# 1280 NO_OPs in the program of TensorE, one behind each group of three large matmuls

## Chip, core and metric

The kernel runs on one core of one Trainium2 chip. The metric is the device time of one execution in microseconds (us). TensorE is called PE below, its weight loads PEld, VectorE DVE, ScalarE ACT, GpSimd POOL and SyncE SP, as the profile does.

## What is computed

One step of a hybrid decoder layer, for 1024 new tokens of one prompt and 8 single new tokens of running sequences. All is float32, with D = 2048 features:

```python
mod = silu(c) @ w_ada + b_ada
shift, scale, gate = split(mod, 3)
h = rmsnorm(x, norm_g) * (1 + scale) + shift
z = h @ w_in                                    # 2048 x 8208
b_a, c_a, h_a, g_a, qkv, g_b, beta_logit, alpha_logit = split(z)
y_a = b_a * causal_conv3(c_a * h_a) * silu(g_a)
q, k, v = split(silu(causal_conv4(qkv)))        # 8 heads of 128, q and k of unit length
o, s = gated_delta_rule(q, k, v, g, beta, s0)   # g, beta from the logits
y = concat(y_a, rmsnorm(o, o_norm_g) * silu(g_b)) @ w_out
x = x + gate * y
```

The outputs are the final RMSNorm of x and the new states of the two convolutions and of the delta rule. Most of the arithmetic is in the two products with w_in and w_out.

## The kernel before

The features lie on the 128 partitions, the tokens on the free axis. The tokens are done in two halves: half 0 is 512 tokens of the prompt, half 1 the other 512 and the 8 single ones. In each half a loop first goes over the 64 column tiles (128 columns each) of w_in, in an order written out by hand (`order`), and then over the 16 column tiles of w_out. In half 1 the tokens are split into two blocks of 264 and 256.

A float32 product is made of three matmuls of a narrower kind (`float32r`). Each operand is split in two, a rounded part (hi) and what is left (lo); `passes` adds hi x hi, lo x hi and hi x lo into one accumulator tile in PSUM. Such a group of three matmuls, for one 128-row piece of the contraction and one block of tokens, is what the change speaks of. In the profile the activations of the products with w_in are called `hh` and `hl`, those with w_out `yhi` and `ylo`, and the weights `whi` and `wlo`. Each matmul has its own weight load in the chip's program, even where two in a row use the same weights.

`product` computes one column tile: 16 pieces of contraction, so 16 groups (48 matmuls) in half 0, and 32 groups in half 1 where there are two blocks. It takes the split weights from a stream (`ws.next`): SP loads 128x512 pieces (`raw`), ACT rounds them (`whi`), and POOL or DVE computes the rest (`wlo`). The first seven column tiles are computed elsewhere, in the phase that computes `mod`, and don't go through `product`.

Between the matmuls of a group `passes` calls `pump`, where small work of other generators is slipped in: transposes, the steps of the delta rule, the gate vectors. A planner (`_Order`) decides this while the kernel is built, from its own account of when each engine is free. That account is told of a matmul by the helper at line 369, `_Tensor.mm`; all matmuls carry line 370 in the profile, all other recorded operations line 321.

What is computed from a column tile leaves PSUM by ACT or DVE; an output tile of w_out in half 0 is read by DVE (`res<-mm,ga,xr`). There are three accumulator tiles (`ps_mm`), so the first matmul of a tile waits for an earlier reader of its place, and for the weights.

Of the kernel before, what the change touches and what calls it, by code (L numbers as in the profile page):

```python
# [77 lines left out]
def trunk_kernel(tc, xT, w_in, w_ada, w_out, pack, consts, vecs, csq, ssm,  # L78
                 yT, cap, cqp, ssp, cas, cqs, sss):
    nc = tc.nc  # L80
    ctx = ExitStack()
    with ctx:
        _trunk(ctx, tc, nc, xT, w_in, w_ada, w_out, pack, consts, vecs, csq, ssm, yT, cap, cqp, ssp, cas, cqs, sss)
# [6 lines left out]
class _Order:  # L90
# [156 lines left out]
    def pump(self):  # L247
        for s in list(self.side):
            if s[0] <= self.now:
                self._step(s)  # L250
# [112 lines left out]
class _Tensor:  # L363
# [5 lines left out]
    def mm(self, out, lhsT, rhs, cost=None, **kw):  # L369
        r = self.pe.matmul(out, lhsT, rhs, **kw)  # L370
        if cost is None:
            n = _size(rhs)
            if rhs.dtype == F32R:
                cost = max(n / 2250.0, 0.05) + 0.004
            elif kw.get("is_transpose"):
                cost = 0.109
            else:
                cost = max(4 * n / 2400.0, 0.21) + 0.006
        self.od.put("P", [lhsT, rhs], [out], cost)
        return r  # L380


def _trunk(ctx, tc, nc, xT, w_in, w_ada, w_out, pack, consts, vecs, csq, ssm, yT, cap, cqp, ssp, cas, cqs, sss):
# [18 lines left out]
    def mm_tile():  # L402
        return ps_mm.tile([P, 512], F32, tag="mm", name="mm")
# [231 lines left out]
    def passes(ps, whi, wlo, hh, hl, a, b, first, last, fill=False):  # L635
        mm(ps[:, :b - a], whi, hh[:, a:b], start=first, stop=False)
        if fill:
            pump()
        mm(ps[:, :b - a], whi, hl[:, a:b], start=False, stop=False)
        if fill:  # L640
            pump()
        mm(ps[:, :b - a], wlo, hh[:, a:b], start=False, stop=last)
        if fill:
            pump()

    def product(w, col, rows, ops, blocks, before=None):


        pss = [mm_tile() for _ in blocks]
        for qi, kq in enumerate(rows):  # L650
            if before:
                before(qi)
            whi, wlo = ws.next((col, kq), ws.used)
            for ps, (a, b) in zip(pss, blocks):
                for j in range(4):
                    hh, hl = ops[kq * 4 + j]
                    passes(ps, whi[:, j, :], wlo[:, j, :], hh, hl, a, b, qi == 0 and j == 0, qi == 3 and j == 3, True)
        return pss


# [599 lines left out]
    def group_a(half, g, blocks, y, pch=None):  # L1260
        n = WH if half else HT
        pc = pch[0] if pch else product(w_in, 1024 + g * P, range(4), hs, blocks)
        hold("ca", 1)
        c_ = tp.tile([P, WH], F32, tag="ca", name="c_", bufs=1)
        for ps, (a, b) in zip(pc, blocks):
            S.activation(c_[:, a:b], ps[:, :b - a], AF.Copy)
        phh = pch[1] if pch else product(w_in, 2048 + g * P, range(4), hs, blocks)
        hold("zr", 2)
        u = tp.tile([P, WH + 3], F32, tag="zr", name="ua")
# [24 lines left out]
        od.spawn(conv())  # L1294
        yield
        pg = pch[2] if pch else product(w_in, 3072 + g * P, range(4), hs, blocks)
        hold("ca", 1)
        gc = tp.tile([P, WH], F32, tag="ca", name="gc", bufs=1)
# [631 lines left out]
```

## Time and profile before

| | |
|---|---|
| time, median of 3 runs | 2162.79 us (2159.91 to 2165.25) |
| the profiled execution | 2164.96 us, span 2163.2 us |
| granted clock of PE, mean | 0.993 |
| PE busy | 2116.0 us, 15045 matmuls |
| PEld busy | 1853.8 us, 15045 weight loads |
| DVE, ACT, POOL busy | 1262.9, 826.3, 835.9 us |

The span goes from the first to the last instruction. The time of a matmul in a row is that of one matmul from its start to its modelled end; matmuls overlap, so how fast they follow each other is read from their starts. Behind a row of the timeline stands, in brackets, for how long the engine was idle and who ended that. PEldq is the sequencer of PE, which hands weight loads and matmuls to the array and carries out what needs no array.

### The profile page before, as it was taken

Reading aid. Unit: us, or ns where it says so; the run is one execution under the profiler, and the core shown is the slowest. Engines: PE = TensorE matmul, PEld = TensorE weight load, DVE = VectorE, ACT = ScalarE, POOL = GpSimd, SP = SyncE. Lnnn points to the kernel's source line nnn. Section 1 sums busy time; section 2 is a strip of 40 time slices with the busy share of each in tenths; the row PEclk is TensorE's granted clock in tenths of the full one; section 3 lists DMA queues with packets and bytes.
Section 4 is the critical chain, followed back from the end, with each engine's and each line's share of the span. In section 5 each row is a group of like instructions: output and inputs, shape, how many; then the busy total and the mean of one; then the engine's idle time right before and its main releaser. Section 6 shows DMA issues by size and latency. Waiting matters only on the chain. (4 is left out here: it accounts for less than half of the span.)

```text
span 2163.2 us, 40436 instructions
## 1 busy us (share of the span) xinstructions
PE 2116.0 (98%) x15045; PEld 1853.8 (86%) x15045; DVE 1262.9 (58%) x3646; ACT 826.3 (38%) x1885; POOL 835.9 (39%) x808
## 2 busy tenths in 40 slices
PE   9899999999999999999999999999999999999996
PEld 6478777777788887778899999999999999999996
DVE  3347776666768645287134865666576487245454
ACT  3234343334444332343233334342443433344553
POOL 0133433333343434323444334344443433444444
PEclk9999999999999999999999999999999999999998
DMA  9974765997445357855445565467574445868776
GB/s 313 340 220 83 161 149 147 134 165 134 115 99 98 89 104 83 82 182 179 142 102 120 107 120 119 113 100 104 107 93 90 89 103 95 92 92 241 228 208 197
DMA packets 466599, 299.66 MB, mean 139 GB/s; under 512 B 37601, under 2 KB 429537, under 8 KB 466401
## 3 DMA queue, kind: packets, MB, share of 16 engines
q1 hardware_dynamic: 442608, 284.26, 61.4%
q10 hardware_dynamic: 23792, 12.81, 2.4%
q8 instruction: 118, 1.93, 0.4%
q14 instruction: 81, 0.66, 0.1%
HBM read 277.06 MB, written 19.94 MB: 137 GB/s over the span
## 5 line engine op out<-in xcount | busy, mean ns | idle before, releaser
L321 POOL TENSOR_TENSOR wlo<-raw,whi 128x512 fp32r<-128x512 f32 x536 | 718.6, 1342 | 1222.7 <-ACT whi L321 1067.6
L370 PE MATMUL mm<-hh,whi 128*128 128x264 f32 (+1 forms) x3008 | 971.6, 323 | 10.9 <-DVE y L321 5.6
L370 PE MATMUL mm<-hl,whi 128*128 128x264 f32 (+1 forms) x3008 | 969.2, 322 | 3.7 <-DVE hl L321 3.7
L370 PE MATMUL mm<-hh,wlo 128*128 128x264 f32 (+1 forms) x3008 | 968.2, 322 | 0.7 <-POOL wlo L321 0.7
L321 ACT ACTIVATE whi<-raw 128x512 fp32r<-128x512 f32 x672 | 418.4, 628 | 617.7 <-PE mm L370 323.8
L370 PEld LDWEIGHTS mm<-hh,whi 128*128 128x128 f32 x3008 | 567.7, 189 | 61.6 <-issue 9.8
L370 PEld LDWEIGHTS mm<-hl,whi 128*128 128x128 f32 x3008 | 568.0, 189 | 47.7 <-DVE hl L321 5.9
L370 PEld LDWEIGHTS mm<-hh,wlo 128*128 128x128 f32 x3008 | 567.8, 189 | 43.6 <-issue 2.5
L370 PE MATMUL mm<-yhi,wlo 128*128 128x512 f32 (+2 forms) x768 | 247.7, 323 | 5.4 <-DVE wlo L321 3.2
L370 PE MATMUL mm<-yhi,whi 128*128 128x512 f32 (+2 forms) x768 | 246.6, 321 | 1.2 <-ACT whi L321 1.2
L370 PE MATMUL mm<-ylo,whi 128*128 128x512 f32 (+2 forms) x768 | 247.1, 322 | 0.0
L321 DVE TENSOR_TENSOR ob<-tb,xb 128x62 f32<-128x62 f32 (+30 forms) x992 | 191.5, 233 | 7.0 <-DMA tb<-ub 7.0
L321 DVE TENSOR_TENSOR xb<-xb,ob 128x62 f32<-128x62 f32 (+30 forms) x992 | 195.5, 237 | 0.0
L321 DVE TENSOR_TENSOR wlo<-raw,whi 128x512 fp32r<-128x512 f32 x136 | 108.2, 802 | 110.4 <-ACT whi L321 106.3
L370 PEld LDWEIGHTS mm<-yhi,wlo 128*128 128x128 f32 x768 | 145.3, 189 | 19.9 <-DVE wlo L321 4.8
L370 PEld LDWEIGHTS mm<-yhi,whi 128*128 128x128 f32 x768 | 145.3, 189 | 12.9 <-ACT whi L321 1.7
L370 PEld LDWEIGHTS mm<-ylo,whi 128*128 128x128 f32 x768 | 145.2, 189 | 12.5 <-issue 1.0
L321 DVE SCALAR_TENSOR_TENSOR kq<-zr,pk,kq 128x512 f32<-128x512 f32 x96 | 105.0, 1094 | 3.4
L321 DVE SCALAR_TENSOR_TENSOR res<-mm,ga,xr 128x512 f32<-128x512 f32 (+2 forms) x48 | 27.3, 568 | 106.1 <-PE mm L370 92.9
L321 DVE TENSOR_TENSOR acc<-acc,sqt 128x512 f32<-128x512 f32 (+3 forms) x70 | 51.3, 736 | 38.2 <-ACT sqt L321 37.3
L321 DVE SCALAR_TENSOR_TENSOR rt<-cht,gt_neg,v 128x128 f32<-128x128 f32 x56 | 19.5, 349 | 78.9 <-PE cht L370 78.8
L321 ACT ACTIVATE u<-cht,sm 128x128 f32<-128x128 f32 x64 | 23.5, 367 | 99.6 <-DVE u L321 95.7
(410 smaller groups left out, 1996.3 us busy)
## 6 DMA issues: line engine op xcount, KB each, us to landing
raw<-in_w_in SPq DMA_DIRECT2D x488, 256.0 KB, 5.1
raw<-in_w_out SPq DMA_DIRECT2D x160, 256.0 KB, 3.3
wat<-in_w_ada SPq DMA_DIRECT2D x64, 512.0 KB, 8.7
gw<-in_w_ada SPq DMA_DIRECT2D x64, 256.0 KB, 6.5
tb<-ub ACTq DMA_DIRECT2D x16, 512.0 KB, 6.1
raw<-in_w_in SPq DMA_DIRECT2D x48, 128.0 KB, 6.7
sl<-in_ssm SPq DMA_DIRECT2D x12, 512.0 KB, 6.1
x1s<-in_xT SPq DMA_DIRECT2D x16, 260.0 KB, 4.8
```

The costliest lines, as they stand in the source:

```text
L321: r = f(*args, **kw)
L370: r = self.pe.matmul(out, lhsT, rhs, **kw)
```

## The change

A list of 1280 entries is made once. In `product`, behind each group of three matmuls, one entry is taken and one instruction that does nothing is put into PE's program, until the list is empty.

```diff
+    spaces = [0] * 1280
+
     def product(w, col, rows, ops, blocks, before=None):
...
                 for j in range(4):
                     hh, hl = ops[kq * 4 + j]
                     passes(ps, whi[:, j, :], wlo[:, j, :], hh, hl, a, b, qi == 0 and j == 0, qi == 3 and j == 3, True)
+                    if spaces:
+                        spaces.pop()
+                        nc.tensor.nop("space", nofuse=True)
         return pss
```

The instruction goes to PE directly, past `_Tensor.mm`, so the planner doesn't know of it. Apart from these 1280 rows every engine has the same instructions in the same order with the same waits as before. Product groups of half 0 take 57 x 16 + 16 x 16 = 1168 of them, the first three and a half tiles of half 1 the other 112.

PE in half 0, in the first tile that goes through `product` (`mm`; the number tells one tile of a name from another, and `tpt` is a small transpose of the logits `zl`), before:

```order
L370 MATMUL mm_1633<-hl_879,whi_1506 128x512
L370 MATMUL tpt_1674<-cs_82,zl_1631 128x16 [waits Activation_49]
L370 MATMUL tpt_1674<-cs_82,zl_1631 128x16 x3
L370 MATMUL mm_1633<-hh_878,wlo_1507 128x512
L370 MATMUL mm_1633<-hh_1096,whi_1524 128x512
L370 MATMUL mm_1633<-hl_1097,whi_1524 128x512
L370 MATMUL mm_1633<-hh_1096,wlo_1525 128x512 [waits Pool_49]
```

The same place in the changed kernel:

```order
L370 MATMUL mm_1633<-hl_879,whi_1506 128x512
L370 MATMUL tpt_1681<-cs_82,zl_1631 128x16 [waits Activation_49]
L370 MATMUL tpt_1681<-cs_82,zl_1631 128x16 x3
L370 MATMUL mm_1633<-hh_878,wlo_1507 128x512
L662 NO_OP
L370 MATMUL mm_1633<-hh_1096,whi_1524 128x512
L370 MATMUL mm_1633<-hl_1097,whi_1524 128x512
L370 MATMUL mm_1633<-hh_1096,wlo_1525 128x512 [waits Pool_49]
L662 NO_OP
```

A NO_OP stands behind each matmul with `wlo` and in front of the next with `whi`; what `pump` slips in stays where it was.

PE in half 0 at the border between two output tiles of w_out, before:

```order
L370 MATMUL mm_10293<-ylo_9357,whi_10294 128x512
L370 MATMUL mm_10293<-yhi_9184,wlo_10295 128x512
L370 MATMUL mm_10374<-yhi_9183,whi_10316 128x512 [waits DVE_49,Activation_49]
L370 MATMUL mm_10374<-ylo_9196,whi_10316 128x512
L370 MATMUL mm_10374<-yhi_9183,wlo_10317 128x512 [waits Pool_49]
```

The same border in the changed kernel:

```order
L370 MATMUL mm_11365<-ylo_10277,whi_11366 128x512
L370 MATMUL mm_11365<-yhi_10080,wlo_11367 128x512
L662 NO_OP
L370 MATMUL mm_11462<-yhi_10079,whi_11392 128x512 [waits DVE_49,Activation_49]
L370 MATMUL mm_11462<-ylo_10092,whi_11392 128x512
L370 MATMUL mm_11462<-yhi_10079,wlo_11393 128x512 [waits Pool_49]
L662 NO_OP
```

The first matmul of a tile waits for two engines, DVE and ACT, as before; the NO_OP stands in front of it and waits for nothing.

PE in half 1, where the list runs out, in the changed kernel (before, the same rows without the NO_OP):

```order
L370 MATMUL mm_12606<-hh_10471,whi_12509 128x256
L370 MATMUL mm_12606<-hl_10472,whi_12509 128x256
L370 MATMUL mm_12606<-hh_10471,wlo_12510 128x256
L662 NO_OP
L370 MATMUL mm_12605<-hh_10707,whi_12548 128x264
L370 MATMUL mm_12605<-hl_10708,whi_12548 128x264
L370 MATMUL mm_12605<-hh_10707,wlo_12549 128x264 [waits Pool_49]
```

From the last row on the program of PE is that of before.

## Prediction

> **What bounds the kernel now.** I read the page first, then the busy time by stage, then the groups and the waits inside the stretch that gets the new instructions, then single instructions there. The page:
>
> ```profile
> span 2163.2 us, 40436 instructions
> PE 2116.0 (98%) x15045; PEld 1853.8 (86%) x15045; DVE 1262.9 (58%) x3646; ACT 826.3 (38%) x1885; POOL 835.9 (39%) x808
> PE   9899999999999999999999999999999999999996
> PEclk9999999999999999999999999999999999999998
> ```
>
> PE is busy in every slice, at its full granted clock; no other engine passes 58%. So anything that lengthens PE's stream reaches the end of the kernel nearly one for one, and anything that doesn't touch it costs nothing. The profiled execution took 2164.96 us, its span 2163.2 us and 1.8 us around it; that is 0.1% above the median of the three runs, 2162.79 us (2159.91 to 2165.25).
>
> The groups of matmuls in the stretch from 160 to 1108 us tell how many groups of three the change follows there:
>
> ```profile
> L370 PE MATMUL mm<-hh,wlo 128*128 128x512 f32 x912 | 365.6, 401 | 0.7 <-POOL wlo L321 0.7
> L370 PE MATMUL mm<-yhi,wlo 128*128 128x512 f32 x256 | 101.0, 395 | 1.9 <-DVE wlo L321 1.9
> ```
>
> Each group of three ends in one matmul with wlo, so 912 + 256 = 1168 of the 1280 instructions stand in the first half of the sequence, and 112 remain for the second: three and a half tiles of 32 groups. By stage (columns: length, then busy time of PE, of its weight loads, DVE, ACT, POOL, the clock, DMA), and the waits of PE from 164 to 1163 us, the first and the last of nine rows, 14 waits together:
>
> ```profile
> 164.20:1107.90 943.70, 934.06 (x4845) 741.68 (x4843) 581.70 (x1680) 356.77 (x802) 353.75 (x330) 1.00 0.62 127
> 1107.90:1163.00 55.10, 55.10 (x463) 54.91 (x463) 26.81 (x52) 27.68 (x65) 25.50 (x28) 1.00 0.38 91
> ...
> PE mm L370 <- DVE wlo L321: 1.9, 2, 1.7
> ...
> PE tpt L370 <- DVE os__8082 L321: 0.3, 1, 0.3
> ```
>
> In 998.8 us PE stands still for 9.6 us. The array is the limit here, not what feeds it.
>
> **The change part by part.** It removes and moves nothing: the order of every engine is as before, no matmul gets another wait, and the new instructions carry none. It adds 1280 instructions to the sequencer of PE, which hands weight loads and matmuls to the array. What counts is whether the sequencer has that time to spare, and whether such an instruction stops it from working ahead.
>
> First the array's pace. These are the last matmuls of one output tile and the first of the next, with the weight load of that first one and the eviction by DVE, which marks where the tile ends:
>
> ```profile
> 1031.44 0.40 PE L370 MATMUL mm<-yhi,whi 128*128 128x512 f32 x1
> 1031.67 0.40 PE L370 MATMUL mm<-ylo,whi 128*128 128x512 f32 x1
> ...
> 1035.38 0.39 PE L370 MATMUL mm<-yhi,wlo 128*128 128x512 f32 x1
> 1035.38 0.19 PEld L370 LDWEIGHTS mm<-yhi,whi 128*128 128x128 f32 x1
> 1035.61 0.40 PE L370 MATMUL mm<-yhi,whi 128*128 128x512 f32 x1
> 1035.81 0.75 DVE L321 SCALAR_TENSOR_TENSOR res<-mm,ga,xr 128x512 f32<-128x512 f32 x1 [8.29 <-PE mm L370]
> ```
>
> From 1031.44 to 1035.61 are 18 steps, 0.232 us each (the 0.40 us of a record overlaps with the next). The load at 1035.38 starts together with the matmul in front of it, so it is hidden. In the second half the products are split:
>
> ```profile
> 1203.02 0.28 PE L370 MATMUL mm<-hh,whi 128*128 128x264 f32 x1
> 1204.47 0.28 PE L370 MATMUL mm<-hh,whi 128*128 128x256 f32 x1
> 1205.90 0.28 PE L370 MATMUL mm<-hh,whi 128*128 128x264 f32 x1
> ```
>
> Twelve steps take 1.45 and 1.43 us, so 0.119 us for the narrower ones. A group of three lasts 0.696 us in the first half and at least 0.357 us in the second.
>
> Then the sequencer's pace. The fastest stream in the trace is the row of tiny warm-up matmuls, each with its weight load:
>
> ```profile
> 0.99 17.27 PE L370 MATMUL cht<-ones 32*32 32x32 f32 x320 [0.99 <-POOL nhalf L321]
> ```
>
> 17.27 / 320 = 0.054 us for a pair at most (the array may be what limits even this). Three pairs cost the sequencer up to 0.162 us. The trace has no NO_OP on PE. The nearest rows are another kind that the sequencer handles alone: the EVENT_SEMAPHOREs that stand in front of a matmul that waits for more than one semaphore (all of them, one at 1031.5, and four in a row just before the first output product):
>
> ```profile
> L370 PEldq EVENT_SEMAPHORE  x133: 51/51/399, 17.1 to 2092.0; - x133
> ...
> L370 PEldq EVENT_SEMAPHORE  x1: 51/51/51, 1031.5 to 1031.5; - x1
> ...
> L370 PEldq EVENT_SEMAPHORE  x4: 51/51/51, 919.3 to 919.7; - x4
> ```
>
> One lasts 0.051 us, and four stand within 0.4 us, so start to start is about 0.13 us. I take 0.051 us for a NO_OP, since it does less, and 0.13 us as the upper end. A group then costs the sequencer 0.213 us, at most 0.292, against 0.696 us of the array (0.357 in the second half). It stays faster than the array everywhere.
>
> The middle row says more. Of the output tiles here, only the first matmul waits for two things, for DVE and for ACT; its EVENT_SEMAPHORE ran at 1031.5 and the matmul itself at 1035.61. The sequencer was 17 matmuls, about 4 us, ahead, with 17 pairs queued behind it. So a sequencer's instruction runs while earlier matmuls are still waiting for the array, and a delay of 0.05 or 0.13 us is paid out of 4 us. **Cover:** those queued pairs hide the cost; where they are gone, right after PE had to wait at an EVENT_SEMAPHORE, a NO_OP could show. PE waits 14 times in the stretch: 14 x 0.13 = 1.8 us as the upper end. But behind such a wait the array first works through the pairs it was just given, so I take 0.1 us. The lower end is 0: no wait, load or matmul is dropped.
>
> Last, the program gets longer, and is fetched by DMA (packets, MB, share of the 16 DMA engines over the span):
>
> ```profile
> q8 instruction: 118, 1.93, 0.4%
> ```
>
> 1.93 MB over 2 x 15045 instructions is 64 bytes each, 16.4 KB a packet. 1280 more are 82 KB, 5 packets. 0.4% of 16 engines over 2163 us, divided by 118, is 1.2 us a packet, one for some 18 us of PE's work. I take 0 for them; if PE stood still for all five, 5 x 1.2 = 6 us.
>
> Sum: 2164.96 + 0.1 = 2165.1 us for an execution like the profiled one, 2162.9 us against the median; I say 2163. With both upper ends it is 2162.8 + 1.8 + 6 = 2170.6 us.
>
> **The rivals.** *In line (slower).* A NO_OP might keep the next weight load from being taken early. What that costs stands where the array was switched from another shape:
>
> ```profile
> 306.09 0.50 PE L370 MATMUL mm<-hh,whi 128*128 128x512 f32 x1
> 306.43 0.39 PE L370 MATMUL mm<-hl,whi 128*128 128x512 f32 x1
> ...
> 306.09 0.19 PEld L370 LDWEIGHTS mm<-hh,whi 128*128 128x128 f32 x1 [0.84 <-issue]
> 306.20 0.19 PEld L370 LDWEIGHTS mm<-hl,whi 128*128 128x128 f32 x1
> ```
>
> The step is 0.34 us instead of 0.23: a load that isn't hidden costs 0.11 us. 1280 x 0.11 = 141 us, 2304 us; with only the 0.051 us of the instruction itself in the path 65 us, 2228 us. It decides once the sequencer's work per group passes 0.696 us in the first half, so from a NO_OP of 0.53 us on, or if it empties the queue. Against it stands the 4 us by which an EVENT_SEMAPHORE ran ahead; for it only that a NO_OP is another opcode.
>
> *Taking turns (slower, little).* The NO_OP waits until the matmul in front of it has begun, then the load follows. Counted from that start: 0.051 for the NO_OP, 0.027 for issuing the load (half a pair), 0.11 for the load, 0.188 us. In the first half that still fits into 0.232 us; in the second it is 0.069 us over, 112 x 0.069 = 7.7 us, 2170.5 us. This is how I read the Trainium skill, "PSUM — Partial Sum Buffer", section "Engine vs sequencer instructions": a nop belongs to the sequencer, which waits for the instructions before it to be dispatched, not to complete. If dispatched means handed to the array, the time would be the 2170.5 us just worked out; if it means put into the queue, there is no cost. The trace bears out the second, with the EVENT_SEMAPHORE at 1031.5, though no run here shows a NO_OP.
>
> *Spreading (faster).* The load behind a NO_OP starts a little later, and the matmul beside it, which now shares its start with a load, runs undisturbed. The steps in the rows above lie at 0.23 us each within 0.01, so at most 1280 x 0.01 = 13 us, 2150 us. With a full queue the array sees no NO_OP, which speaks against any of it.
>
> *Nothing arrives.* The instructions could be dropped on the way to the chip: 2162.8 us, the same verdict.
>
> **How the numbers follow.** 0.3%, 6.5 us, is about what a measurement of this kernel can tell from no change. Hidden 0.81 and nothing arrives 0.02, both within it: 0.83. Taking turns 0.05 and in line 0.08, both slower by more: 0.13. Spreading 0.04, faster. The predicted time is that of the hidden case. The range goes from 2157 us, somewhat below the lowest of the runs shown, to 2172 us, which takes in the upper ends of the sum and the case of taking turns, with the scatter of a run; in line and most of spreading, 0.12 or less, are left out.
>
> **What would show it.** Right: 1280 NO_OPs on PE, each about 51 ns; the step of 0.232 us unchanged across a NO_OP; PE busy in the first stretch within 2 us of 934 in some 944 us; EVENT_SEMAPHOREs of the output products still about 4 us ahead; 123 packets of instructions. Wrong: steps of 0.28 or 0.34 us behind every third matmul from 172 to 1108 us (in line), the first half alike but a loss of some 8 us before 1163 us (taking turns), or a step that shrinks (spreading).

## The result, and the profile after

The changed kernel takes 2260.45 us (median of 4 runs, 2259.24 to 2269.74), the kernel before 2164.02 us on the same chip (4 runs, 2159.91 to 2167.03): ratio 1.0454, 95% interval 1.0438 to 1.0471. It is 96 us slower; the prediction was 2163 us, no change.

The page of the changed kernel, the rows that answer to those of before:

```profile
span 2257.5 us, 41716 instructions
PE 2151.6 (95%) x15045; PEld 1875.7 (83%) x15045; DVE 1246.4 (55%) x3646; ACT 824.8 (37%) x1885; POOL 836.5 (37%) x808
PE   8999998999999989999999989999999899999997
PEclk9999999999999989999999999999999999999998
...
q8 instruction: 123, 2.02, 0.4%
...
raw<-in_w_in SPq DMA_DIRECT2D x488, 256.0 KB, 6.2
```

PE now has slices with holes. And a row moved that nothing in the change touches: the loads of w_in took 6.2 us from issue to landing, where before it was

```profile
raw<-in_w_in SPq DMA_DIRECT2D x488, 256.0 KB, 5.1
```

**The NO_OPs themselves.** All instructions on line 662 of the changed kernel (count, duration in ns as min/median/max, first and last start), and the last matmuls of the output tile of w_out that the prediction quoted from before, with the first of the next:

```profile
L662 PEldq NOP  x1280: 13/13/13, 167.6 to 1205.9; - x183
```

```profile
1085.58 0.40 PE L370 MATMUL mm<-yhi,whi 128*128 128x512 f32 x1
1085.81 0.40 PE L370 MATMUL mm<-ylo,whi 128*128 128x512 f32 x1
1086.05 0.39 PE L370 MATMUL mm<-yhi,wlo 128*128 128x512 f32 x1
1086.27 0.40 PE L370 MATMUL mm<-yhi,whi 128*128 128x512 f32 x1
...
1089.52 0.39 PE L370 MATMUL mm<-yhi,wlo 128*128 128x512 f32 x1
1089.75 0.40 PE L370 MATMUL mm<-yhi,whi 128*128 128x512 f32 x1
```

A NO_OP lasts 13 ns. Behind every `wlo` row now stands one, and the steps from 1085.58 to 1089.75 are still 18 in 4.17 us, 0.232 us each, across a NO_OP (1086.05 to 1086.27) as elsewhere. The EVENT_SEMAPHORE in front of the new tile still runs some 4 us ahead:

```profile
L370 PEldq EVENT_SEMAPHORE  x1: 51/51/51, 1085.7 to 1085.7; - x1
```

Setting the start of each NO_OP beside that of the last matmul of its group, it ran a median of 17 matmuls and 3.1 us ahead.

**Where the time went.** The changed kernel by stage, cut at the same matmuls as before (columns as in the prediction), and under it the rest of the second half before:

```profile
162.80:1162.10 999.30, 959.30 (x4846) 756.00 (x4845) 572.91 (x1681) 355.53 (x802) 353.19 (x335) 0.97 0.60 120
1162.10:1217.00 54.90, 54.90 (x462) 54.71 (x462) 26.97 (x51) 27.45 (x65) 25.89 (x28) 1.00 0.44 89
1217.00:2257.50 1040.50, 985.36 (x8545) 966.62 (x8543) 584.52 (x1800) 393.84 (x941) 424.34 (x412) 0.98 0.61 123
```

```profile
1163.00:2163.20 1000.20, 973.36 (x8543) 958.30 (x8542) 591.71 (x1800) 393.70 (x941) 423.07 (x412) 0.99 0.63 128
```

The two profiled executions differ by 94 us in span. The first stretch grew from 943.7 to 999.3 us, the last from 1000.2 to 1040.5 us, where no NO_OP stands: 40 of the 94 us lie behind the last one. The stretch between them, with its NO_OPs among the short matmuls, took 54.90 us after 55.10. In the first stretch PE stands still for 999.30 - 959.30 = 40.0 us where it was 9.6, and in the last for 55.1 where it was 26.8; it is also busy for 25 and 12 us longer with the same matmuls, at a lower mean clock (0.97 for 1.00 and 0.98 for 0.99).

PE waits for two things: for pieces of weights, and for the small work that is slipped in between the matmuls. In these stretches the waits whose end the profile names come to 83.3 us, and before to 25.0 us. Of these, 18.0 us were ended by `whi` or `wlo` (before 7.1), nearly all the rest by other work of ACT and DVE, most of it the small work. The first three rows of the changed kernel (us in all, times, longest):

```profile
PE tpt L370 <- ACT sp L321: 11.2, 3, 6.1
PE mm L370 <- ACT whi L321: 9.0, 8, 2.2
PE mm L370 <- POOL wlo L321: 7.4, 9, 1.8
```

First the weights. The idle time of ACT in front of `whi` that a load of w_in ended (columns as above), changed kernel and then before:

```profile
ACT whi L321 <- DMA raw<-in_w_in: 265.1, 94, 9.2
```

```profile
ACT whi L321 <- DMA raw<-in_w_in: 123.0, 50, 8.0
```

One place where this reaches PE, in the changed kernel: four roundings of pieces of w_in (in brackets the idle time of ACT and what ended it), and then PE, which needs the last of them.

```profile
789.54 0.63 ACT L321 ACTIVATE whi<-raw 128x512 fp32r<-128x512 f32 x1 [5.05 <-DMA raw<-in_w_in]
...
795.66 0.63 ACT L321 ACTIVATE whi<-raw 128x512 fp32r<-128x512 f32 x1 [4.97 <-DMA raw<-in_w_in]
799.29 0.63 ACT L321 ACTIVATE whi<-raw 128x512 fp32r<-128x512 f32 x1 [3.01 <-DMA raw<-in_w_in]
...
805.41 0.63 ACT L321 ACTIVATE whi<-raw 128x512 fp32r<-128x512 f32 x1 [3.52 <-DMA raw<-in_w_in]
```

```profile
804.00 0.40 PE L370 MATMUL mm<-hh,wlo 128*128 128x512 f32 x1
806.10 0.50 PE L370 MATMUL mm<-hh,whi 128*128 128x512 f32 x1 [1.70 <-ACT whi L321]
...
807.47 0.63 PE L370 MATMUL mm<-hh,whi 128*128 128x512 f32 x1
807.90 0.63 PE L370 MATMUL mm<-hl,whi 128*128 128x512 f32 x1
808.33 0.63 PE L370 MATMUL mm<-hh,wlo 128*128 128x512 f32 x1
```

The same four before:

```profile
748.75 0.63 ACT L321 ACTIVATE whi<-raw 128x512 fp32r<-128x512 f32 x1 [1.77 <-DMA raw<-in_w_in]
...
752.12 0.63 ACT L321 ACTIVATE whi<-raw 128x512 fp32r<-128x512 f32 x1 [2.21 <-DMA raw<-in_w_in]
753.17 0.63 ACT L321 ACTIVATE whi<-raw 128x512 fp32r<-128x512 f32 x1 [0.42 <-DMA raw<-in_w_in]
...
756.07 0.63 ACT L321 ACTIVATE whi<-raw 128x512 fp32r<-128x512 f32 x1 [0.29 <-DMA raw<-in_w_in]
```

A piece serves four groups, which keep PE busy for 12 x 0.232 = 2.8 us. Before, the four came within 7.3 us, 2.4 us apart, so the feed kept up by a little; now within 15.9 us, 5.3 us apart, and when the stock of ready weights is used up, PE stands. There is a second charge: behind the wait the steps are 0.43 us (807.47, 807.90, 808.33) and no longer 0.232. The clock that was granted there:

```profile
806.80:809.00 2.20, 2.15 (x6) 1.74 (x6) 0.03 (x1) 0.00 (x0) 0.00 (x0) 0.50 0.63 54
```

It is 0.50; from 800 to 806 us it had been 1.00. Matmul by matmul, some 27 of the 94 us lie in about 155 steps that became 0.1 to 0.4 us longer, about 135 of them with the matmul itself over a quarter longer, as at a lowered clock; 37 steps longer by over 0.4 us, the waits themselves, hold 70 us; waits that became shorter and small differences make up the rest. The Trainium skill, "TensorE: Matmul & The Clock Gate", section "Part 1: The HAM clock gate", states that an idle window of about 3.4 us drops the array to half clock, with 427 ns for a step of 512 columns. The half clock and the 0.43 us agree; the length doesn't, as this wait had 1.7 us of idleness in one piece and was enough, behind a stretch of 21 us in which PE had stood still for 5.2 us:

```profile
785.00:806.00 21.00, 15.77 (x54) 11.22 (x54) 1.87 (x6) 4.87 (x15) 3.95 (x4) 0.84 0.65 57
```

Then the small work. The longest wait of PE in the changed kernel, 6.06 us, was not ended by a piece of weights: ACT stood still for `xd<-xb`, a transfer of 64 KB of the small work.

```profile
353.11 1.31 PE L370 MATMUL tpt<-sp 128*128 128x256 f32 x2 [6.06 <-ACT sp L321]
```

```profile
352.42 0.63 ACT L321 ACTIVATE sp<-kq 128x512 fp32r<-128x512 f32 x1 [8.44 <-DMA xd<-xb]
```

**Which loads.** I gave each load of 256 KB its column tile by the order in the code. Median time from issue to landing in us, by number of the column tile modulo 8, 64 loads each (40 in class 2, whose other loads are smaller):

```text
class                  0     1     2     3     4     5     6     7
before               7.9   5.0   4.2   4.9   4.4   4.1   4.8   9.8
changed             14.8   7.1   6.1   4.6   7.3   4.1   5.1   6.0
```

Before, classes 0 and 7 were slow. The kernel's author knew: line 292 is `SLOW = (0, 7)`, and `_transfer` gives such a load 66 GB/s. In the changed kernel class 0 takes twice as long, 1, 2 and 4 are slower and 7 is quicker. A load of `raw` reads 512 rows of w_in, 512 bytes of each, 32,832 bytes apart, so the column tile says where in each row, and the class where within 8 x 512 = 4096 bytes.

What is transferred beside a slow load lands late too. Median landing in us of three transfers of the small work, with a load of a slow class in flight when they were issued (0 and 7 before, 0 in the changed kernel; 5 to 12 cases each) and with only loads of other classes:

```text
                     before, slow   other     changed, slow   other
ub<-dU, 16 KB             6.3        3.1           11.2        3.5
xd<-xb, 64 KB             8.2        4.3           11.8        4.5
dA<-gcd, 256 KB           8.9        4.4           16.3        6.6
```

In the wait of 6.06 us above, `xd<-xb` took 10.0 us, beside loads of class 4 that took 7 to 10. So slower loads reach PE by two ways, as weights that come late and as small work that comes late. How the 94 us split between them, no run here shows.

### The profile page after: what moved, and what is told of

Read it like the earlier page. It is cut to its first block, busy times and chain, and to the rows that moved or that the text cites. A ratio compares the mean times of both kernels' runs of the same rounds, so it can differ in the third digit from the quotient of the medians.

```text
span 2257.5 us, 41716 instructions
## 1 busy us (share of the span) xinstructions
PE 2151.6 (95%) x15045; PEld 1875.7 (83%) x15045; DVE 1246.4 (55%) x3646; ACT 824.8 (37%) x1885; POOL 836.5 (37%) x808
## 5 line engine op out<-in xcount | busy, mean ns | idle before, releaser
L370 PE MATMUL mm<-hh,whi 128*128 128x264 f32 (+1 forms) x3008 | 981.5, 326 | 25.4 <-ACT whi L321 8.8
L370 PE MATMUL mm<-hh,wlo 128*128 128x264 f32 (+1 forms) x3008 | 979.7, 326 | 5.4 <-POOL wlo L321 5.0
L370 PE MATMUL mm<-hl,whi 128*128 128x264 f32 (+1 forms) x3008 | 979.1, 325 | 4.0 <-DVE hl L321 4.0
L370 PEld LDWEIGHTS mm<-hh,whi 128*128 128x128 f32 x3008 | 574.8, 191 | 80.2 <-ACT whi L321 12.0
L370 PEld LDWEIGHTS mm<-hh,wlo 128*128 128x128 f32 x3008 | 575.2, 191 | 54.6 <-POOL wlo L321 9.1
L370 PEld LDWEIGHTS mm<-hl,whi 128*128 128x128 f32 x3008 | 575.3, 191 | 49.1 <-DVE hl L321 6.2
```

## The experiments

Theory *placement*: 1280 instructions of 64 bytes make PE's program 81,920 bytes longer, the arrays lie 81,920 bytes further in the chip's memory, and how fast a load of w_in is depends on where its rows lie. Rival *cost per NO_OP*: 96 us / 1280 = 0.075 us for each one, in the sequencer or in the fetch.

### The same NO_OPs late, in another engine, and twice as many

Late: the 1280 stand behind the last 1280 groups (against the changed kernel).

```diff
-    spaces = [0] * 1280
+    grp, SKIP = [0], 2448
...
-                    if spaces:
-                        spaces.pop()
+                    grp[0] += 1
+                    if grp[0] > SKIP:
                         nc.tensor.nop("space", nofuse=True)
```

> The same 1280 instructions on PE, but behind the last 1280 groups of three (all in the second half of the sequence, from about 1650 us on) instead of the first 1280. Placement theory (PE's longer program moves what the DMA reads to another place in HBM, so that other column tiles of w_in load slowly): the time of the changed kernel, 2260 us within 10, with some 54 us lost before 1110 us, where no NO_OP stands, and class 0 of the column tiles (tile number modulo 8) the slow one, its loads landing after some 14 us. Rival (the NO_OPs hold PE or its feed up where they stand, 96 / 1280 = 0.075 us each): the first half as before, w_out reached at the same time as before, and the whole loss after 1650 us.

Measured: 2266.98 us (before 2164.42, 13 runs), ratio 1.048 (1.0462 to 1.0497). Its NO_OPs, and a stretch of the first half:

```profile
L662 PEldq NOP  x1280: 13/13/13, 1717.6 to 2249.2; - x183
```

```profile
160.00:1040.00 880.00, 838.69 (x4317) 658.32 (x4316) 531.02 (x1617) 319.46 (x744) 306.59 (x299) 0.97 0.61 115
```

PE idles for 41 us from 160 to 1040 us, though the first NO_OP runs at 1717.6 us, and class 0 lands in 14.4 us, as in the changed kernel. At the matmul that began at 1031.4 us before, this kernel is 56.0 us late and the changed one 54.1 us. The NO_OPs don't cost where they stand.

In DVE's program (against the kernel before):

```diff
+    spaces = [0] * 1280
...
+                    if spaces:
+                        spaces.pop()
+                        nc.vector.nop("space", nofuse=True)
```

> The same 1280 instructions in the program of DVE instead of PE, at the same places of the build. Placement theory, if the programs of all engines lie in one region ahead of the weights: about the changed kernel's 2260 us, since the programs are longer by the same 81,920 bytes; if PE's program alone matters, before's time. Rival (the cost is paid on PE for each NO_OP): PE has none, so 2164 us, at most some 10 us more for DVE.

Measured: 2165.0 us, ratio 1.0004 (0.9994 to 1.0013); the classes land as before (0 in 7.8, 7 in 9.4 us). A longer program of DVE has no such effect. It is fetched elsewhere: the packets of the queue q8, 118 before and 123 in the changed kernel, stay at 118, and those of q14, the other queue of instructions, go from 81 to 90 (0.66 to 0.74 MB). Why PE's program moves w_in and this one doesn't, no run here shows.

Twice as many on PE (against the changed kernel):

```diff
-    spaces = [0] * 1280
+    spaces = [0] * 2560
...
-                    if spaces:
+                    for _ in range(min(2, len(spaces))):
```

> Two NO_OPs behind each of the first 1280 groups, 2560 in all. Rival (cost per NO_OP): twice the loss, 2164 + 192 = 2356 us. Placement theory: no proportion to the number; another place in HBM, with its own slow column tiles, so any time from 2150 to 2300 us, and the step between matmuls still 0.232 us across two NO_OPs.

Measured: 2287.54 us, ratio 1.0569 (1.0552 to 1.0585). Twice the NO_OPs cost 123 us and not 192; class 0 lands in 15.5 us, 1 in 7.8, 2 in 7.0. The loss doesn't go by their number, and the median step from a `wlo` matmul of the first half to the next `whi`, across two NO_OPs, is still 0.232 us.

### The shift without a NO_OP

w_in lies 81,920 bytes behind the start of a longer input. Every engine has the instructions, the order and the waits of the kernel before.

```diff
+PAD = 20480
...
-            ("w_in", f["w_in"][0]),
+            ("w_in", np.concatenate([np.zeros(PAD, np.float32), f["w_in"][0].reshape(-1)])),
...
+        if name == "w_in":
+            args[-1] = bass.AP(args[-1].tensor, PAD, [[8208, D], [1, 8208]])
```

> No NO_OP at all; w_in itself is moved in HBM: it lies 81,920 bytes behind the start of its input, which is longer by as much. Every engine has the instructions of before in the same order with the same waits. Placement theory: other slow column tiles than 0 and 7 modulo 8 and another time than before, near 2260 us if w_in alone counts and moves by just this much. Rival: 2164 us, classes 0 and 7 slow as before.

Measured: 2259.43 us, ratio 1.0441 (1.0426 to 1.0457). Its page and the waits of ACT (its lines are numbered one higher; the planner's table is applied to the shifted columns, so that the order stays):

```profile
span 2258.1 us, 40436 instructions
PE 2152.7 (95%) x15045; PEld 1876.9 (83%) x15045; DVE 1247.4 (55%) x3646; ACT 825.4 (37%) x1885; POOL 833.4 (37%) x808
...
raw<-in_w_in SPq DMA_DIRECT2D x488, 256.0 KB, 6.2
```

```profile
ACT whi L322 <- DMA raw<-in_w_in: 255.2, 93, 8.1
```

With the 40436 instructions of before, it has the span, PE time and landing of the changed kernel, and its classes: 14.0, 7.3, 5.7, 4.4, 7.2, 4.2, 5.3 and 6.2 us. At that same matmul it is 53.7 us late. This is the whole loss without a NO_OP; the rival falls. Whether arrays behind w_in moved with it, the trace, which has no addresses, can't tell.

### A small shift, both ways

First PAD = 4096, so 16,384 bytes, without NO_OPs (against the shift above); then only 256 NO_OPs, 16,384 bytes of program (against the changed kernel):

```diff
-PAD = 20480
+PAD = 4096
```

```diff
-    spaces = [0] * 1280
+    spaces = [0] * 256
```

> No NO_OP; w_in begins 16,384 bytes behind the start of its input, as far as one packet of 1/5 of the added program. Placement of w_in: the classes move by some amount between those of before and those of the changed kernel, so a time off 2164 us, which I can't say better than 2160 to 2260 us. Cost per NO_OP: 2164 us.

> Only the first 256 NO_OPs, 16,384 bytes of program. Placement of w_in: the time and the landing of every class agree with those of the kernel without NO_OPs in which w_in begins 16,384 bytes later, within 5 us. Cost per NO_OP: 2164 + 256 x 0.075 = 2183 us, whatever that other kernel takes.

Measured, against 2165.14 us of before (19 runs): 2164.66 us, ratio 1.0 (0.999 to 1.0009), and 2165.62 us, ratio 1.001 (0.9999 to 1.002). The classes:

```text
class                  0     1     2     3     4     5     6     7
shift of 16,384      9.1   5.1   4.4   4.4   4.9   4.0   4.8   8.5
256 NO_OPs           9.0   5.2   4.6   4.5   4.7   4.0   4.6   8.4
```

What the two have in common against before is the 16,384 bytes, and every class agrees within 0.2 us; both differ from before (7.9 and 9.8 us in classes 0 and 7). So a longer program of PE acts as a shift of w_in by as many bytes, here and at 81,920. A small shift hands some of class 7's delay to class 0, and the order still holds that.

### Undoing the shift by a larger one

The changed kernel, with w_in another 966,656 bytes behind the start of its input, 1 MiB together (the other lines as in the shift of 81,920 bytes).

```diff
+PAD = 241664
```

> All 1280 NO_OPs stand where the change put them, and w_in begins 966,656 bytes behind the start of a longer input, so that together with the 81,920 bytes of the longer program it lies exactly 1 MiB from its old place. Placement of w_in: if only the address below 1 MiB decides which loads are slow, the time is back at 2164 us with the NO_OPs still in, and the median landing of column class 0 back at about 8 us; if higher bits count too, some third pattern and time. Cost per NO_OP: 2260 us, since every NO_OP is still there.

Measured: 2232.34 us, ratio 1.0313 (1.0298 to 1.0329): neither. The undoing failed, since the slow classes are now 3 and 4 (10.5 and 8.1 us; the others 4.1 to 4.9), half a turn from 0 and 7. If the bytes add up to 1 MiB as they should, the part of the address from 1 MiB up counts too. The run tells something else: these loads are on the whole about as fast as before (median 4.9 us against 5.1), only other ones are slow, and the kernel is 67 us slower. It is not the weights here: ACT waits less for loads than before (123.0 us in 50 waits), and PE's waits for `whi` and `wlo` come to 4.8 us (before 7.1). PE waits for small work. PE's longest row and that of ACT:

```profile
PE tpt L371 <- ACT sp L322: 17.7, 3, 11.2
```

```profile
ACT whi L322 <- DMA raw<-in_w_in: 107.3, 42, 5.8
```

With a load of class 3 or 4 in flight, `xd<-xb` lands in 8.8 us, otherwise in 3.0. The kernel's `order` fits that: it puts the four tiles of a class in a row for the classes 1, 3, 4, 5 and 6 (`h(3) + ...`), and deals those of 0 and 7 out one at a time between others (`h(7, 0) + a(3, 0) + h(7, 1)`). So the order seems fitted to which tiles come late; no run here changes the order.

### The planner told of the new slow class

```diff
-SLOW = (0, 7)
+SLOW = (0,)
```

> The changed kernel with its 1280 NO_OPs and w_in where they push it, but the planner's table names class 0 alone as slow, since class 7 lands in 5 to 6.5 us there. If the loss comes from an order made for the wrong classes: some of the 96 us comes back, 2200 to 2245 us. If it comes from loads that are too slow whatever the order: 2250 to 2270 us. Cost per NO_OP: 2260 us.

Measured, in the changed kernel: 2257.77 us against 2161.37 of before (13 runs), ratio 1.0439 (1.041 to 1.0467). That lies in the expected range for loads that are too slow whatever the order, but the cost per NO_OP would give it too: the table alone brings back nothing to speak of, though ACT's waits for loads went from 265.1 to 196.6 us. The table enters only the planner's account of time; the order of the column tiles is written by hand, and class 0 still takes 13.8 us.

### Other pitches

w_in with its rows padded from 8208 to 8320 floats, 33,280 bytes apart in place of 32,832; instructions, order and waits as before.

```diff
+PITCH = 8320
...
-    if src.tensor.name == "in_w_in" and int(src.offset) % 8208 // P % 8 in SLOW:
+    if src.tensor.name == "in_w_in" and int(src.offset) % PITCH // P % 8 in SLOW:
...
-            ("w_in", f["w_in"][0]),
+            ("w_in", np.pad(f["w_in"][0], ((0, 0), (0, PITCH - 8208)))),
```

> The kernel before, but the rows of w_in are padded from 8208 to 8320 floats (a pitch of 33,280 bytes, 65 x 512), the order of the work and the planner's table unchanged. Placement of w_in: the pieces of a column tile then lie otherwise in HBM; if the slow classes come from the old pitch of 32,832 bytes, classes 0 and 7 land in 4 to 5 us like the others and the time is 2150 to 2166 us, as PE had only some 10 us of waits left to lose; if the new pitch falls badly, other classes or all are slow and the time is above 2200 us. Cost per NO_OP has nothing to say here: 2164 us.

Measured: 2152.57 us, ratio 0.9942 (0.9927 to 0.9957), 0.6% faster than before. On its page:

```profile
PE 2107.7 (98%) x15045; PEld 1849.7 (86%) x15045; DVE 1265.0 (59%) x3646; ACT 826.1 (38%) x1885; POOL 840.1 (39%) x808
...
raw<-in_w_in SPq DMA_DIRECT2D x488, 256.0 KB, 2.9
```

Every class lands in 2.9 or 3.0 us, where 4 to 5 were expected, and the small transfers with them (`ub<-dU` 2.4, `xd<-xb` 2.8, `dA<-gcd` 3.9 us beside a load of w_in). ACT's idle time in front of `whi` that a load of w_in ended, 123.0 us in 50 waits before:

```profile
ACT whi L322 <- DMA raw<-in_w_in: 7.9, 2, 7.7
```

Then this pitch with the 1280 NO_OPs of the change in it:

```diff
+    spaces = [0] * 1280
...
+                    if spaces:
+                        spaces.pop()
+                        nc.tensor.nop("space", nofuse=True)
```

> The padded pitch of 33,280 bytes, in which every load landed in 2.9 us, with all 1280 NO_OPs of the change in PE's program. Placement of w_in: with no slow class there is nothing that a shift of 81,920 bytes can make worse, so the time is that of the padded kernel without NO_OPs, 2152.6 us, within 5 us, and all classes land in about 3 us. Cost per NO_OP: 2152.6 + 96 = 2249 us.

Measured: 2154.30 us (2151.34 to 2155.82), ratio 0.996 (0.9944 to 0.9976). The first stretch, between the same matmuls, without the NO_OPs and with 1168 of them:

```profile
162.70:1099.80 937.10, 932.07 (x4846) 742.38 (x4845) 583.81 (x1680) 356.55 (x802) 356.19 (x330) 1.00 0.43 128
```

```profile
166.90:1104.00 937.10, 932.04 (x4846) 742.24 (x4844) 583.78 (x1680) 356.53 (x802) 356.55 (x330) 1.00 0.43 128
```

937.10 us both times. Where no load is slow, the shift does no harm and the NO_OPs are free: the cost that the prediction gave them was right.

Is it the alignment? 33,280 is a multiple of 512 bytes, 32,832 only of 64. So the next has rows of 8336 floats, 33,344 bytes, a multiple of 64 alone:

```diff
-PITCH = 8320
+PITCH = 8336
```

> Rows padded to 8336 floats, 33,344 bytes: as far from the old pitch as the good one was, but like the old one a multiple of 64 bytes and not of 512, so that a piece of 512 bytes lies across two lines of 512 in seven rows of eight. If the good pitch works by its alignment: landing stays at 4 to 5 us or more and slow classes are seen, 2160 us or above. If it works by spreading the rows otherwise: about 3 us in all classes and 2152 us.

Measured: 2155.83 us, ratio 0.9972 (0.9963 to 0.9982), all classes in 2.9 or 3.0 us. Not the alignment: 512 bytes more from row to row suffice. And the first good pitch with an empty table:

```diff
-SLOW = (0, 7)
+SLOW = ()
```

> The padded pitch, and the planner told of no slow class (the table of two classes emptied), so that it orders small work and loads for a feed that is even. If the wrong table still costs something: 2140 to 2150 us. If the order was no longer what PE waits for: 2152.6 us within 3 us. It could be worse, since the order was written by hand for the old table: up to 2165 us.

Measured: 2150.36 us, ratio 0.9945 (0.993 to 0.996), not to be told from the same pitch with the old table.

That the rows of the old pitch, 32 KiB and 64 bytes apart, crowd into few parts of the memory, and that the start of w_in decides which column tiles crowd most, fits all of this; the trace names no address and no part of the memory, so it is argued and not shown. The Trainium skill, "DMA: Bandwidth & Descriptors", section "Latency and other measured facts", has copies that slow down at row pitches of 2 MiB and more, gives crowded channels as an inference, and pads by 4 KiB, where 192 bytes did not help. Here the pitch is far smaller, it matters where the array begins, and 448 bytes are enough.

## Why the prediction was wrong

- *The array's pace and the cover*: right. The steps are 0.232 us across a NO_OP, the sequencer is 17 matmuls ahead as it was, and two stretches of 937.10 us show the cost as nothing. A NO_OP takes 0.013 us where 0.051 was taken; being hidden, that changed nothing.
- *In line*: fell, though its 2228 to 2304 us hold the time that was measured. The steps behind the NO_OPs aren't the 0.28 or 0.34 us that it asked for: from a `wlo` matmul of the first half to the next `whi` the median is 0.232 us, and at the even pitch 54 of 1098 such steps exceed 0.27 us with the NO_OPs and 54 without. That its range holds the measured time is chance. *Taking turns*: fell, as the stretch of short matmuls went from 55.10 to 54.90 us. The rule of the Trainium skill cited there ("PSUM — Partial Sum Buffer", "Engine vs sequencer instructions") is to be read the second way: what is put into the queue counts as dispatched, and the lead of 17 matmuls agrees. *Spreading* and *nothing arrives*: fell.
- *"It removes and moves nothing"*: this step failed, and with it *"I take 0 for them; if PE stood still for all five, 5 x 1.2 = 6 us"*. The five packets came (123 in all) and cost nothing as a fetch. But the longer program was priced only as something to fetch, not as something that takes up room. It acted as if w_in lay 81,920 bytes further, which turned class 0 from 7.9 to 14.8 us a load and cost 96 us; the shift alone gives 2259.43 us for 2260.45. None of the rivals had the place of the data in it.
- *"The array is the limit here, not what feeds it"*, and with it *"anything that doesn't touch it costs nothing"*: true of the trace and taken too far. The 9.6 us of waits were a balance: ACT already waited 123.0 us for loads, in the slow classes pieces came 2.4 us apart for 2.8 us of work, and the transfers of the small work landed in 6 to 9 us beside a slow load. That the speed of a load hung on the column tile stood in the kernel at line 292; I read the table as a planner's rule and didn't ask what would change it.
- *What would show it*: "PE busy within 2 us of 934 in some 944" was the row that broke, 959.30 in 999.30; the NO_OPs' count, the packets, the steps and the lead of the EVENT_SEMAPHORE came as said.

## What to carry to other kernels

Where a kernel's order is fitted to how long its loads take, ask of every change, even one that does nothing, whether it moves an array in memory; to tell a cost of instructions from one of placement, shift the array alone and leave the program as it was. Look at landing times by place and not by their median over all: 5.1 us hid loads of 10 us beside loads of 4. And look at every transfer that is in flight beside such loads: in the version with 1 MiB the weights came in time, and 67 us were lost all the same. A pitch at which all loads are alike (2.9 us) is worth more than an order written around the late loads, and here it held when the program grew by 81,920 bytes.

## What the runs showed of the hardware

- A NO_OP on PE takes 13 ns and is carried out while a median of 17 matmuls and their weight loads, 34 instructions, still wait for the array.
- 1280 more instructions in PE's program act as a shift of w_in by 81,920 bytes (256 as one of 16,384); 1280 in DVE's don't.
- A load of 512 pieces of 512 bytes took 2.9 to 3.0 us (medians of each class) at pitches of 33,280 and 33,344 bytes, and between 4 and 15.5 us, by column tile and by where the array begins, at 32,832.
- A transfer of 16 KB took 11.2 us with a slow load in flight, 3.5 us with other loads and 2.4 us at the even pitch.
- A wait of PE costs more than its length: behind one with 1.7 us of idleness steps of 0.232 us became 0.43 us at a granted clock of 0.50.
